# Interleaving scores and transposes in the attention of a hybrid decoder block, with smaller edits at the start, in the parameters and at the end

## The chip, the cores and the metric

The kernel runs on one core of one Trainium2 chip. The metric is the device time of one execution in microseconds (us), the median of several runs. All tensors are fp32. The core has a matrix engine (TensorE, "PE" in the profile, with its weight loads listed as "PEld"), VectorE (DVE), ScalarE (ACT), GpSimd (POOL) and SyncE (SP), which here only issues DMAs.

## The reference

The reference is one layer over 512 tokens of width 1024. Of it, what bears on the change:

```python
xn = rmsnorm(x, norm_g)                       # 512 x 1024
u  = xn @ w_in                                # all column groups of one projection
# mLSTM branch: q, k get a causal depthwise convolution of width 4 + SiLU; 4 heads of 256
q, k = silu(conv(u_q, conv_q_w, conv_q_b)), silu(conv(u_k, conv_k_w, conv_k_b))
ya = head_layernorm(mlstm(q, k, v, i, f)) * mh_norm_g * ...
# sparse attention branch: 8 heads of 64, 2 key groups; rotary angles on the first 16 of 64 dims
q, ks, kw = rope(u_nq), rope(u_nks), rope(u_nkw)
for each head, each of two key sets (selected, window):
    P = softmax(causal(q k^T / 8));  yb += gate * (P @ v)
yb += gate * compressed attention over 31 blocks
# both branches: silu gate, branch projection, sigmoid merge, one output projection
out = rmsnorm(x + merged @ w_out, final_norm_g)
```

The attention here is dense and causal for both key sets: 512 tokens fit in the window and in the selected blocks.

## The kernel before, in words

A matrix product of two fp32 matrices is done as three passes in TensorE's rounded fp32 format: each operand is split into a high part (a rounding copy, mostly on ACT) and a low part (a subtraction on DVE), and high x high, low x high and high x low are added up in one PSUM bank. `split` does this for one tile; names that end in `h` and `l` are the two parts. Weights arrive as `wr` (or `R`, `T`) and become `wh` and `wl`; `hTh` and `hTl` are the two parts of the normalized input, transposed.

The program has five stretches. From 0 to 26 us (first stage): four blocks of 128 tokens, `xts[0..3]`, are loaded; for each, `stats` finds the factor `r` of the norm (ACT squares, POOL power), `normed(tb, half)` scales half a block on DVE in place (`xt`), `turned` transposes it on TensorE, `high` and `low` split it. In between, a small projection (`small_hi`, `small_lo` split its weights `sraw` into `shi` and `slo`; `some_of` are its matmuls) gives value rows and gate columns, which `evacuate` takes out of PSUM. From 26 to 205 us: the projections for values and the gate paths, with sums for a Winograd scheme, and fitted into them two small jobs. `params` loads the convolution weights, the norm gains, the position table `cpos` and the positions, and transposes them on TensorE so that they lie along partitions (eight transposes of 11 rows into `prm`, two more). `angles` builds cosines and sines of the rotary angles, pads them to 128 columns a token block and transposes them (eight transposes of 128 by 128) into `Ct` and `St`, which the rotation of queries and keys reads from about 203 us on. From 205 to 380 us: the attention. From 380 to 525 us the mLSTM, from 525 us the branch and output projections, and the end.

The attention has 16 units (`units`: four pairs of heads, two heads, two key sets) of `NT` = 4 query blocks. For a block `qb`, `score` makes two matmuls into a `ps` bank (there are two), and `softmax_block` takes the minimum of the negated scores on DVE (the custom instruction) and the exponential with its sum on ACT, into the tile `P`. After a unit's last block DVE makes the reciprocal of the four sums and the gate (`st`), and POOL scales the four blocks of `P` (line 1058). `ptrans(P, kb)` then transposes key block `kb` of `P` for the query blocks that see it: 4, 3, 2, 1 transposes for `kb` 0 to 3, into a `pt` bank (there are two), which `split` copies to `pth` (ACT) and `ptl` (DVE). `pvmul` multiplies both by the values into the `po` bank (one), and `collect` takes a head's result out.

Between these, `tick(n)` runs `n` passes (the three-pass products' matmuls `pp<-hTh,wh`, `hTl,wh`, `hTh,wl`, 512 columns each) of a `stream` of other column projections, and one step of each side job (`compressed`, `mgate`). These "fill" matmuls are needed anyway: what is not done here is done by `stream.drain()` after the attention. The order on TensorE is the order of the code; ACT's, DVE's and POOL's is set by a scheduler that the program runs at build time, which is why rows are compared in the built program further down. All ACT, DVE and PE instructions carry the line of one recording helper, L75.

The loop of a unit: four times (score of the next unit, three fill passes, one late product), then four times (one `ptrans` of this unit, three fill passes, and the product that is `LAG` = 3 behind).

At the end, per token block, `join` adds a PSUM bank to `xo`, `square` squares it on ACT with a sum into `fs`, `more` adds the sum to `fb` on POOL, `factor` makes the power -1/2 in `fr` on POOL, and `times` (DVE, by the gain `late`), `scaled` (ACT, by `fr`) or `both` (DVE, one instruction for the two) give the output, which is stored.

Of the kernel before, what the change touches and what calls it, by code (L numbers as in the profile page):

```python
# [19 lines left out]
D = 1024  # L20
# [7 lines left out]
LAG = 3  # L28
# [30 lines left out]
def build(  # L59
# [45 lines left out]
    cpos = pers.tile([128, 32], F32, name="cpos")  # L105
# [6 lines left out]
    mhalf = pers.tile([128, 4], F32, name="mhalf")  # L112
# [120 lines left out]
    prm = pers.tile([128, 8, 11], F32, name="prm")  # L233
# [9 lines left out]
    vD = dram.tile([128, NT, D], F32, name="vD")  # L243
    gD = {
# [10 lines left out]
    posT = tiny[:, 256:260]  # L255
# [30 lines left out]
    with tc.tile_pool(name="ph0", bufs=2, side="right") as p0, tc.tile_pool(  # L286
# [8 lines left out]
        act.preload_act_table_set("natural_log_exp_and_others")  # L295
        ordered.add("pe")
# [12 lines left out]
        nc.sync.dma_start(cst[:, :CTRI], consts[:, :CTRI])  # L309
# [53 lines left out]
        bif = sp.tile([128, 8], F32, name="bif")  # L363
        bng = sp.tile([128, 24], F32, name="bng")
# [4 lines left out]
        def evacuate(tb, ps):  # L369
            pv = ps[:, 0:256].rearrange("p (b g d) -> p b g d", b=2, g=2)  # L370
            for b in range(2):
                split(pv[:, b], vsw[:, tb, b, :, 0, :], vsw[:, tb, b, :, 1, :])
            dve.tensor_tensor(gp[:, tb, 0:24], ps[:, 256:280], bng, OP.add)
            dve.tensor_tensor(gp[:, tb, 24:32], ps[:, 280:288], bif, OP.add)
# [44 lines left out]
        lo4, hi4 = range(4), range(4, 8)  # L419
        normed(0, 0)  # L420
# [4 lines left out]
        stats(1)  # L425
# [5 lines left out]
        low(0, 0)  # L431
# [5 lines left out]
        low(0, 1)  # L437
        small_hi(6, "p")
        high(1, 0)
        high(1, 1)  # L440
        small_hi(4, "a")
        small_lo(0)
        small_lo(2)
        low(1, 0)
        low(1, 1)
        some_of(0, "lh", lo4)
        some_of(1, "hh", lo4)
        some_of(0, "hh", hi4)
        some_of(0, "lh", hi4)
        some_of(1, "hh", hi4)  # L450
# [3 lines left out]
        some_of(1, "lh", hi4)  # L454
        whole(0, 0)
        whole(0, 1)
        stats(2)
        small_lo(6)
        small_lo(4)
        some_of(0, "hl", (6, 7, 4, 5), stop=True)  # L460
        some_of(1, "hl", (6, 7, 4, 5), stop=True)
        whole(1, 0)
        whole(1, 1)
        stats(3)
        nc.sync.dma_start(bif[:, 0:4], b_igate[0].partition_broadcast(128))
        nc.sync.dma_start(bif[:, 4:8], b_fgate[0].partition_broadcast(128))
        nc.sync.dma_start(bng, b_nsa_gate[0].partition_broadcast(128))
        for hf in range(2):
            normed(2, hf)
            turned(2, hf, PT())  # L470
        three = idle, PS()
        for hf in range(2):
            normed(3, hf)
            turned(3, hf, three[hf])
        vq = quarters(vview, ((0, 0), (1, 0)))
        for tb in (2, 3):
            for hf in range(2):
                high(tb, hf)
                low(tb, hf)
            if tb == 2:  # L480
                evacuate(0, sums[0])
# [5 lines left out]
        for tb in (2, 3):  # L487
            some_of(tb, "hh", lo4)
            some_of(tb, "hl", lo4)
            some_of(tb, "hh", hi4)  # L490
            some_of(tb, "hl", hi4)
            some_of(tb, "lh", lo4)
            some_of(tb, "lh", hi4, stop=True)
# [144 lines left out]
    def params():  # L638
        nc.sync.dma_start(cst[:, CTRI:], consts[:, CTRI:])
        rows = wn.tile([128, D], F32, name="zt", tag="zt")[:11]  # L640
        crow = tiny[:32, 384:512]
        pi = tiny[:4, 512:640].bitcast(I32)
        nc.sync.dma_start(pi, positions[0].rearrange("(a b) -> a b", a=4))
        nc.sync.dma_start(crow[0:16, :], cmp_pos_k[0].rearrange("(a b) d -> a (b d)", b=2))
        nc.sync.dma_start(crow[16:32, :], cmp_pos_v[0].rearrange("(a b) d -> a (b d)", b=2))
        r0 = 0
        for a in (conv_q_w, conv_q_b, conv_k_w, conv_k_b, mh_norm_g):
            src = a[0] if len(a.shape) == 3 else a
            nc.sync.dma_start(rows[r0 : r0 + src.shape[0], :], src)
            r0 += src.shape[0]  # L650
# [5 lines left out]
        pf = tiny[:4, 0:128]  # L656
        dve.tensor_copy(pf, pi)
        pe.transpose(ps[:, 128:132], pf, ident[:4, :4])
        dve.tensor_copy(prm, ps[:, 0:88].rearrange("p (k r) -> p k r", k=8))
        dve.tensor_scalar(prm[:, :, 10], prm[:, :, 10], 0.25, None, OP.mult)  # L660
        dve.tensor_copy(cpos, ps[:, 96:128])
        dve.tensor_copy(posT, ps[:, 128:132])

    def angles():
# [16 lines left out]
        for cc in (c1, c2, c3):  # L681
# [4 lines left out]
        pads = wn.tile([128, D], F32, name="zt", tag="zt")  # L686
        cpad, spad = (
            pads[:, o : o + 512].rearrange("p (b g d) -> p b g d", b=NT, g=2) for o in (0, 512)
        )
        pool.memset(cpad, 1.0)  # L690
        pool.memset(spad, 0.0)
        for g in range(2):
            for o in (0, 8):
                dve.tensor_copy(cpad[:, :, g, o : o + 8], sc[:, 1])
                dve.tensor_scalar(spad[:, :, g, o : o + 8], sc[:, 0], 1.0 if o else -1.0, None, OP.mult)
# [883 lines left out]
```

## Time and profile before

| | |
|---|---|
| runs of the kernel before | median 615.88 us of 3 (615.53 to 616.04) |
| the profiled execution | 615.5 us, of which 613.7 us span, 1.8 us around it |
| granted TensorE clock, mean | 0.997 |
| busy: PE / PEld / DVE / ACT / POOL | 599.9 / 499.6 / 483.7 / 344.1 / 61.8 us |
| attention, steady part 245 to 360 us | PE busy 113.61 of 115 us, DVE 85.51, ACT 72.39, POOL 26.63 |

The profile gives one execution. The time of an instruction in a row is from its start to its modelled end; matmuls are pipelined, so a matmul starts while the one before still shows as busy, and the distance of two starts is what a matmul costs TensorE. A bracket behind a row ("0.60 <-DVE ptl") is the idle time of that engine ahead of the instruction and the work that ended it.

### The profile page before, as it was taken

How to read it: one execution, taken by the hardware profiler on the slowest of the kernel's cores; microseconds unless marked ns; L12 is line 12 of the kernel's file. 1: busy time of each engine (PE TensorE's matmuls, PEld its weight loads, DVE VectorE, ACT ScalarE, POOL GpSimd, SP SyncE). 2: the span in 40 equal slices, each digit the busy share in tenths (PEclk: the TensorE clock that was granted, in tenths of full speed). 3: DMA queues.
4: the chain of work that ended last, by engine and by line, in shares of the span. 5: the costliest groups of instructions: out<-in, count | busy, mean ns of one | idle time of the engine just before them, and what ended most of it. 6: DMA issues, size and time to landing. Idle time of an engine off the chain costs nothing.

```text
span 613.7 us, 8639 instructions
## 1 busy us (share of the span) xinstructions
PE 599.9 (98%) x3024; PEld 499.6 (81%) x3024; DVE 483.7 (79%) x920; ACT 344.1 (56%) x641; POOL 61.8 (10%) x127
## 2 busy tenths in 40 slices
PE   8999999999999999999999999999999999999995
PEld 7988888888888877787878877888787878888884
DVE  6789898596686577885966586889898997589984
ACT  6664556564442356575756575565656563434564
POOL 3000000000100003222121212000000000010122
PEclk9999999999999999999999999999999999999998
DMA  7956554402068361323223222432232234990623
GB/s 223 361 156 187 172 155 137 138 0 87 18 171 219 78 172 57 87 57 85 57 69 91 65 68 87 119 88 69 69 116 92 78 90 127 308 254 18 206 52 139
DMA packets 83052, 73.99 MB, mean 121 GB/s; under 512 B 5072, under 2 KB 64628, under 8 KB 83008
## 3 DMA queue, kind: packets, MB, share of 16 engines
q1 hardware_dynamic: 81854, 70.81, 39.1%
q0 software_dynamic: 1008, 2.36, 2.1%
q8 instruction: 24, 0.39, 0.3%
q10 hardware_dynamic: 146, 0.27, 0.1%
q14 instruction: 20, 0.16, 0.1%
HBM read 61.23 MB, written 8.39 MB: 113 GB/s over the span
## 4 chain that ended last, share of the span: by engine, by line
PE 75%; DVE 15%; ACT 4%; issue 3%; POOL 2%; DMA 1%; POOLq 0%; DVEq 0%; SPq 0%; ACTq 0%
PE pp L75 43%; PE ps L75 18%; PE pt L75 10%; PE po L75 3%; DVE u L75 3%; DVE wl L75 2%; ACT wh L75 1%; DVE P L75 1%; DVE ptl L75 1%; POOL P L1058 1%; ACT P L75 1%; DVE xo L75 1%; DVE num L75 1%; DVE qkl L75 1%; DVE Th L75 1%
## 5 line engine op out<-in xcount | busy, mean ns | idle before, releaser
L75 PE MATMUL pp<-hTh,wh 128*128 128x512 f32 (+1 forms) x360 | 143.5, 399 | 0.0
L75 PE MATMUL pp<-hTl,wh 128*128 128x512 f32 (+1 forms) x360 | 140.0, 389 | 0.0
L75 PE MATMUL pp<-hTh,wl 128*128 128x512 f32 (+1 forms) x360 | 139.4, 387 | 0.0
L75 ACT ACTIVATE wh<-wr 128x1024 fp32r<-128x1024 f32 x56 | 59.0, 1057 | 58.3 <-PE pp L75 52.4
L75 DVE TENSOR_TENSOR wl<-wr,wh 128x1024 fp32r<-128x1024 f32 x56 | 68.2, 1219 | 19.1 <-ACT wh L75 19.0
L75 PEld LDWEIGHTS pp<-hTh,wl 128*128 128x128 f32 x360 | 67.7, 188 | 13.3
L75 PEld LDWEIGHTS pp<-hTh,wh 128*128 128x128 f32 x360 | 68.0, 189 | 10.5
L75 PEld LDWEIGHTS pp<-hTl,wh 128*128 128x128 f32 x360 | 68.0, 189 | 9.4
L1058 POOL TENSOR_SCALAR P<-P,st 128x128 f32<-128x128 f32 (+1 forms) x64 | 36.5, 590 | 157.1 <-DVE st L75 117.4
L75 DVE TENSOR_TENSOR wl<-T,wh 128x1024 fp32r<-128x1024 f32 x28 | 34.0, 1219 | 11.3 <-ACT wh L75 11.3
L75 DVE TENSOR_TENSOR ptl<-pt,pth 128x512 fp32r<-128x512 f32 (+1 forms) x64 | 30.2, 485 | 14.2 <-ACT pth L75 13.8
L75 ACT ACTIVATE P<-P,st 128x128 f32<-128x128 f32 (+3 forms) x64 | 35.5, 554 | 9.9 <-DVE st L75 9.2
L75 ACT ACTIVATE pth<-pt 128x512 fp32r<-128x512 f32 (+1 forms) x64 | 26.9, 434 | 24.6 <-PE pt L75 13.4
L75 DVE TENSOR_TENSOR wl<-R,wh 128x1024 fp32r<-128x1024 f32 x28 | 33.7, 1219 | 8.5 <-ACT wh L75 8.3
L75 DVE CUSTOM_DVE_ANT_0 P<-ps,cst 128x128 f32<-128x128 f32 (+3 forms) x64 | 30.4, 486 | 12.0 <-PE ps L75 11.7
L75 ACT ACTIVATE wh<-T 128x1024 fp32r<-128x1024 f32 x28 | 29.4, 1056 | 18.1 <-PE pp L75 11.0
L75 ACT ACTIVATE wh<-R 128x1024 fp32r<-128x1024 f32 x28 | 29.2, 1058 | 13.3 <-PE pp L75 5.8
L75 DVE SCALAR_TENSOR_TENSOR u<-pp,prm,u 128x511 f32<-128x511 f32 (+2 forms) x48 | 35.6, 742 | 0.4 <-ACT u L75 0.2
L75 PE MATMUL pt<-cst,P 128*128 128x128 f32 x160 | 29.0, 278 | 2.2 <-DVE ptl L75 1.1
L75 PEld LDWEIGHTS pt<-cst,P 128*128 128x128 f32 x160 | 19.7, 140 | 13.8 <-DVE ptl L75 7.5
L75 PE MATMUL ps<-k,Th 128*128 128x256 f32 (+2 forms) x112 | 28.9, 341 | 0.2 <-DVE st L75 0.2
L75 PE MATMUL pp<-yah,wh 128*128 128x512 f32 x64 | 25.0, 391 | 0.0
(350 smaller groups left out, 1348.0 us busy)
## 6 DMA issues: line engine op xcount, KB each, us to landing
wr<-w_in SPq DMA_DIRECT2D x44, 512.0 KB
R<-w_in SPq DMA_DIRECT2D x24, 512.0 KB
gD<-sg SPq DMA_DIRECT2D x16, 256.0 KB
s<-gD SPq DMA_DIRECT2D x16, 256.0 KB
wr<-w_branch_a SPq DMA_DIRECT2D x8, 512.0 KB
R<-w_out SPq DMA_DIRECT2D x8, 512.0 KB
vD<-cq SPq DMA_DIRECT2D x8, 256.0 KB
wr<-vD SPq DMA_DIRECT2D x4, 512.0 KB
```

The costliest lines, as they stand in the source:

```text
L75: ins = fn(*args, **kw)
L1058: pool.tensor_scalar(pj, pj, st[:, 2, j : j + 1], 1.0, OP.mult, OP.mult)
```

## The change

Four parts.

**Attention.** One loop over blocks in place of one over units with two inner loops: a score block, three fill passes, one `ptrans`, three fill passes, one product. The `ptrans` belongs to the block `NT + BEHIND` = 6 steps back, and products follow their transposes by `LAG` = 1 (2 where a head's bank is new). `P` has four buffers in place of three. In the last quarter of the scores one fill pass fewer is run per step, so that 12 passes move behind the attention (102 there, 90 before). The compressed attention's job waits six steps in place of three before its transposes, and the next pair's queries are begun in units 3, 7 and 11.

**Parameters.** The rows are loaded as one tile of 124 rows by 128, turned by one transpose, and `prm` becomes [128, 128] with the position table and the -1/2 constants in it. The cosines and sines are packed without padding (`cc`, 32 columns a token block), turned by one transpose, copied to SBUF by ACT, written to a DRAM tile `csD`, and read back into rows of `Ct` and `St` by four DMAs on SP's queue. `Ct` and `St` are filled with ones and zeros by POOL.

**First stage.** The load of the constants moves from SP's queue to ACT's; block 1 is normed straight after block 0; the small projection's matmuls stand in another order, with block 2's transposes ahead; three bias tiles become one and `evacuate` has one split and one add.

**End.** The last square with its sum is one DVE instruction (`last_factor`), which starts from `fb`, so that POOL goes straight to the power. Token block 0's second half is multiplied by the gain on DVE and scaled on ACT, in place of `both` on DVE; token block 1's second half is one `both` in place of two instructions.

```diff
-LAG = 3
+LAG = 1
+BEHIND = 2
+YIELDS = 6
...
-            at.tile([128, 1280], F32, name="P", tag="P", bufs=3),
+            at.tile([128, 1280], F32, name="P", tag="P", bufs=4),
...
-        for qb in range(NT):
-            if i + 1 < 16:
-                score(*units[i + 1], qb, pair)
-            tick()
-            if late:
-                late.popleft()()
-        for kb in range(NT):
-            tt = ptrans(cur[0], kb)
-            tick()
...
-            late.append(apply)
-            if len(late) > LAG:
-                late.popleft()()
+    for n in range(NT, last + NT + BEHIND):
+        u, m = n // NT, n - NT - BEHIND
...
+        if n < last:
+            scores(n)
+        tick(FILL - 1 if 3 * last // 4 <= n < last else FILL)
+        if m >= 0:
+            apply = values_of(m)
             tick()
+            late.append(apply)
+            while len(late) > (LAG + 1 if m % (2 * NT) == 1 else LAG):
                 late.popleft()()
...
-        for k in range(8):
-            pe.transpose(ps[:, k * 11 : (k + 1) * 11], rows[:, k * 128 : (k + 1) * 128], ident[:11, :11])
-        pe.transpose(ps[:, 96:128], crow, ident[:32, :32])
...
-        pe.transpose(ps[:, 128:132], pf, ident[:4, :4])
+        dve.tensor_copy(rows[96:100], pi)
+        pe.transpose(ps[:, :124], rows, ident[:124, :124])
...
-        for src, dst in ((cpad, Ct), (spad, St)):
-            ps = PP()
-            for tb in range(NT):
-                pe.transpose(
-                    ps[:, tb * 128 : (tb + 1) * 128], src[:, tb].rearrange("p g d -> p (g d)"), ident
-            A(dst, ps, AF.Copy)
+        ps, turned = PP(), tiny[:, 384:512]
+        pe.transpose(ps[:, :128], tiny[:, 512:640], ident)
+        A(turned, ps[:, :128], AF.Copy)
+        nc.sync.dma_start(csD, turned)
+        rows = csD.rearrange("(b r) t -> r b t", b=NT)
+        for g in (0, 64):
+            for r, dst in ((0, Ct), (16, St)):
+                nc.sync.dma_start(
+                    dst[g : g + 16].rearrange("p (b t) -> p b t", b=NT), rows[r : r + 16]
...
-        nc.sync.dma_start(cst[:, :CTRI], consts[:, :CTRI])
+        keep(nc.scalar.dma_start(cst[:, :CTRI], consts[:, :CTRI]))
...
+        stats(1)
         normed(0, 0)
         turned(0, 0, PT())
         warm(3)
         normed(0, 1)
         turned(0, 1, PT())
-        stats(1)
...
-        low(0, 0)
         normed(1, 0)
...
+        def last_factor(tb, cs, n):
+            xv, j = xo[:, tb, cs], junk[:, tb * 2 + n % 2, : cs.stop - cs.start]
+            v = fs[:, tb, n : n + 1]
+            dve.tensor_tensor_reduce(
+                out=j, in0=xv, in1=xv, scale=1.0 / D, scalar=fb[:, tb : tb + 1],
+                op0=OP.mult, op1=OP.add, accum_out=v,
+            )
+            keep(pool.tensor_tensor(fr[:, tb : tb + 1], v, mhalf[:, 0:1], OP.pow))
...
+        times(0, R)
         factor(0, 1)
         more(1, 1)
-        times(1, R0)
         scaled(0, L)
+        scaled(0, R)
         product((None, Y[2]), "MS4", w3, False, tbs=(1,), cs=halves_of[1])
         join(1, R1, Y[2][:, halves_of[1]])
-        square(1, R1, 2)
-        both(0, R)
-        store(0, R)
-        factor(1, 2)
+        last_factor(1, R1, 2)
         scaled(1, L, nc.scalar)
-        both(1, R1)
-        dve.tensor_scalar(xo[:, 1, R0], xo[:, 1, R0], fr[:, 1:2], None, OP.mult)
+        both(1, R)
         store(1, R)
```

In the built programs the recording helper is line 75 before and line 77 after. TensorE in the middle of the attention, before: the four groups of transposes of one unit (`pt<-cst,P`) with their fill.

```order
L75 MATMUL pt<-cst,P 128x128 x4
L75 MATMUL pp<-hTh,wh 128x512
L75 MATMUL pp<-hTl,wh 128x512
L75 MATMUL pp<-hTh,wl 128x512
L75 MATMUL pt<-cst,P 128x128 x3
L75 MATMUL pp<-hTh,wh 128x512
L75 MATMUL pp<-hTl,wh 128x512
L75 MATMUL pp<-hTh,wl 128x512
L75 MATMUL pp<-hTh,wh 128x512
L75 MATMUL pt<-cst,P 128x128 x2
```

The same engine and place in the changed kernel, with a product (`po`) and a score block (`ps`) between two groups of transposes.

```order
L77 MATMUL pt<-cst,P 128x128 x4
L77 MATMUL pp<-hTh,wh 128x512
L77 MATMUL pp<-hTl,wh 128x512
L77 MATMUL pp<-hTh,wl 128x512
L77 MATMUL po<-pth,vsw 128x128
L77 MATMUL po<-ptl,vsw 128x128
L77 MATMUL ps<-k_1609,Th 128x512
L77 MATMUL ps<-k_1610,Th 128x512
L77 MATMUL pp<-hTh,wh 128x512
L77 MATMUL pp<-hTl,wh 128x512
L77 MATMUL pp<-hTh,wl 128x512
```

Between two groups of transposes stood three or four fill passes; now stand six, a product and a score block. The product ahead of that score belongs to the unit before.

VectorE in the first stage, before (after its memsets): the norm of block 0, a low part, the norm of block 1.

```order
L75 SCALAR_TENSOR_TENSOR xt<-xt,r,ps 128x512 x2
L75 TENSOR_TENSOR hTl<-pt,hTh 128x4x128
L75 SCALAR_TENSOR_TENSOR xt<-xt,r,ps 128x512 x2
L75 TENSOR_TENSOR hTl<-pt,hTh 128x4x128
L75 TENSOR_TENSOR slo<-sraw,shi 128x576 x2
```

The same place now:

```order
L77 SCALAR_TENSOR_TENSOR xt<-xt,r,ps 128x512 x4
L77 TENSOR_TENSOR hTl<-pt,hTh 128x4x128
L77 TENSOR_TENSOR slo<-sraw,shi 128x576
L77 TENSOR_TENSOR hTl<-pt,hTh 128x4x128
L77 TENSOR_TENSOR slo<-sraw,shi 128x576
```

The four norm instructions stand together, and the first low part behind them.

VectorE's last instructions before:

```order
L75 SCALAR_TENSOR_TENSOR xo<-pp,xo 128x256
L75 TENSOR_TENSOR xo<-xo,late 128x256
L75 SCALAR_TENSOR_TENSOR xo<-pp,xo 128x256
L75 SCALAR_TENSOR_TENSOR xo<-xo,fr,late 128x512
L75 SCALAR_TENSOR_TENSOR xo<-xo,fr,late 128x256
L75 TENSOR_SCALAR xo<-xo,fr 128x256
```

And now, with the square and its sum as the two ISA rows:

```order
L77 SCALAR_TENSOR_TENSOR xo<-pp,xo 128x256
L77 TENSOR_TENSOR xo<-xo,late 128x512
L77 SCALAR_TENSOR_TENSOR xo<-pp,xo 128x256
L77 ISA junk,fs<-xo,fb 128x256
L77 ISA fs 128x1
L77 SCALAR_TENSOR_TENSOR xo<-xo,fr,late 128x512
```

The gain multiplication ahead of the last join is twice as wide, the square has come to VectorE, and one full-width instruction is left behind it.

More of the change, by code (lines that the diff above doesn't have):

```diff
@@ L110, in build @@
     ident = cst[:, CI : CI + 128]
-    mhalf = pers.tile([128, 4], F32, name="mhalf")
+    prm = pers.tile([128, 128], F32, name="prm")
+    cpos, posT, mhalf = prm[:, 0:32], prm[:, 96:100], prm[:, 124:128]
     pool.memset(mhalf, -0.5)
@@ L370, in evacuate @@
             pv = ps[:, 0:256].rearrange("p (b g d) -> p b g d", b=2, g=2)
[L371 to L374, printed above, removed]
+            split(pv, vsw[:, tb, :, :, 0, :], vsw[:, tb, :, :, 1, :])
+            dve.tensor_tensor(gp[:, tb], ps[:, 256:288], bias, OP.add)
         stats(0)
@@ L441, in build @@
         small_hi(4, "a")
+        small_hi(6, "p")
+        low(0, 0)
         small_lo(0)
+        low(0, 1)
         small_lo(2)
@@ L454, in build @@
         some_of(1, "lh", hi4)
+        stats(2)
         whole(0, 0)
         whole(0, 1)
[L457 to L461, printed above, removed]
+        stats(3)
         whole(1, 0)
         whole(1, 1)
[L464 to L467, printed above, removed]
-        for hf in range(2):
[L469 to L481, printed above, removed]
+        for o, b in ((0, b_nsa_gate), (24, b_igate), (28, b_fgate)):
+            nc.sync.dma_start(bias[:, o : o + b.shape[1]], b[0].partition_broadcast(128))
+        vq = quarters(vview, ((0, 0), (1, 0)))
+        normed(2, 0)
+        turned(2, 0, PT())
+        high(2, 0)
+        small_lo(4)
+        some_of(0, "hl", (4, 5))
+        some_of(1, "hl", (4, 5))
+        small_lo(6)
+        some_of(0, "hl", (6, 7), stop=True)
+        some_of(1, "hl", (6, 7), stop=True)
+        normed(2, 1)
+        turned(2, 1, PT())
+        high(2, 1)
+        some_of(2, "hh", lo4)
+        normed(3, 0)
+        turned(3, 0, idle)
+        some_of(2, "hh", hi4)
+        normed(3, 1)
+        turned(3, 1, PS())
+        low(2, 0)
+        low(2, 1)
+        evacuate(0, sums[0])
+        for hf in range(2):
+            high(3, hf)
+            low(3, hf)
         w1 = hilo(vq[0, 0])
@@ L487, in build @@
         for tb in (2, 3):
[L488 removed]
+            if tb == 3:
+                some_of(tb, "hh", lo4)
+                some_of(tb, "hh", hi4)
             some_of(tb, "hl", lo4)
[L490 removed]
             some_of(tb, "hl", hi4)
@@ L685, in angles @@
         A(sc, ang, AF.Sin)
[L686 to L695, printed above, removed]
+        cc = tiny[:, 512:640].rearrange("p (b r) -> p b r", b=NT)
+        for o in (0, 8):
+            dve.tensor_copy(cc[:, :, o : o + 8], sc[:, 1])
+            dve.tensor_scalar(cc[:, :, 16 + o : 24 + o], sc[:, 0], 1.0 if o else -1.0, None, OP.mult)
+        pool.memset(Ct, 1.0)
+        pool.memset(St, 0.0)
         A(gates, gp[:, :, 0:24], AF.Tanh, scale=0.5)
@@ L1013, in compressed @@
         dve.tensor_tensor(sc, sc, c01.unsqueeze(2).broadcast_to([128, NT, 2, 32]), OP.mult)
-        yield
-        yield
-        yield
+        for _ in range(YIELDS):
+            yield
         ptc = PP()
@@ L1105, in build, with scores @@
     side.append(compressed(0))
-    pair = new_p(), new_p()
-    for qb in range(NT):
-        score(*units[0], qb, pair)
+    pairs_ = {}
+    def scores(n):
+        u, qb = divmod(n, NT)
+        if u % 2 == 0 and qb == 0:
+            pairs_[u // 2] = new_p(), new_p()
+        score(*units[u], qb, pairs_[u // 2])
+    for n in range(NT):
+        scores(n)
         tick(START_FILL)
```

90 lines of the change are left out of this document (42 added, 48 removed).

## The prediction

> **What bounds the kernel now.** I read the page's busy shares first, then the busy time by stretch, then the waits of one stretch, then single stalls in the timeline.
>
> ```profile
> PE 599.9 (98%) x3024; PEld 499.6 (81%) x3024; DVE 483.7 (79%) x920; ACT 344.1 (56%) x641; POOL 61.8 (10%) x127
> ...
> 26.00:208.00 182.00, 182.00 (x869) 152.63 (x869) 143.47 (x204) 95.47 (x129) 3.04 (x11) 1.00 0.46 134
> 208.00:245.00 37.00, 35.67 (x176) 28.03 (x175) 25.74 (x70) 21.52 (x52) 4.88 (x8) 1.00 0.42 113
> 245.00:360.00 115.00, 113.61 (x615) 93.05 (x614) 85.51 (x230) 72.39 (x181) 26.63 (x47) 1.00 0.27 73
> ```
>
> The columns are the stretch, its length, busy time of PE, PEld, DVE, ACT and POOL, the clock and DMA. TensorE has no idle time from 26 to 208 us, at a clock of 1.00, and little elsewhere. So the time is TensorE's: it falls only by a matmul that goes, a stall that goes, or work before the first and after the last matmul. In the attention, the two waits of TensorE that the change aims at are these (us in total, times, longest):
>
> ```profile
> PEld pt L75 <- DVE ptl L75: 7.3, 16, 1.0
> ...
> PEld pt L75 <- POOL P L1058: 1.5, 4, 0.5
> ```
>
> The first row is of 245 to 360 us, the second of 208 to 245. They are waits of the weight load, and part of each is covered by the matmul that still streams. The longest one shows how much:
>
> ```profile
> 276.88 0.40 PE L75 MATMUL pp<-hTh,wl 128*128 128x512 f32 x1
> 277.12 0.40 PE L75 MATMUL pp<-hTh,wh 128*128 128x512 f32 x1
> 278.11 0.44 PE L75 MATMUL pt<-cst,P 128*128 128x128 f32 x2 [0.60 <-DVE ptl L75]
> ...
> L75 ACT ACTIVATE pth<-pt 128x512 fp32r<-128x512 f32 (+1 forms) x64 | 26.9, 434 | 24.6 <-PE pt L75 13.4
> L75 DVE TENSOR_TENSOR ptl<-pt,pth 128x512 fp32r<-128x512 f32 (+1 forms) x64 | 30.2, 485 | 14.2 <-ACT pth L75 13.8
> ```
>
> A 512-column matmul costs 277.12 - 276.88 = 0.24 us from start to start, though its row says 0.40. Here the next start came 0.99 us later, so 0.75 us were lost of a wait of 1.0. TensorE waited for the third group of transposes, because there are two `pt` banks and the first was not yet read out: ACT's copy (0.43 us on average) and DVE's subtraction (0.49 us), one after the other and each behind other work, took longer than the transposes and the four fill passes in between.
>
> **The attention.** Loss now in the middle: 7.3 - 16 x 0.24 = 3.5 us, if each wait is covered by one matmul's 0.24. In the changed order a bank is used again after six fill passes for each of two steps, with a score and a product: by the count of matmuls in the built program times 0.24 us, 3.5 to 5.5 us after its transposes, in place of 1.6 to 2.0. These stalls go: -3.5 us. Outside this stretch (start and tail of the attention) TensorE idles 37 - 35.67 = 1.3 us and a little, part of it on POOL.
>
> What is late next? First, products now follow their transposes after 2.8 to 3.4 us (nine fill passes and a score, by the same count) against 3.4 to 4.8 before; the split needs 0.43 + 0.49 us, and with what is queued ahead up to about twice or three times that, so a few will be late by tenths: I give back 0.4. Second, the start of the attention: the first unit's scaling ends when it ends, and fewer matmuls stand ahead of its transposes: 0.5 given back. Third, the tail, where POOL has least time: 0.4. Net 3.5 - 1.3 = 2.2 us, between 0 (all of it becomes other waits) and 4.5 (also the 1.3 us of the first part go, and nothing is given back less 0.3).
>
> The give-backs rest on POOL's chain from a unit's last score to its first transposes:
>
> ```profile
> 323.52 0.68 PE L75 MATMUL ps<-k,Th 128*128 128x512 f32 x2
> ...
> 324.48 0.68 DVE L75 CUSTOM_DVE_ANT_0 P<-ps,cst 128x512 f32<-128x512 f32 x1
> ...
> 325.20 0.72 ACT L75 ACTIVATE P<-P,st 128x512 f32<-128x512 f32 x1 [0.53 <-DVE st L75]
> ...
> 326.05 0.18 DVE L75 RECIPROCAL st<-st 128x4 f32<-128x4 f32 x1 [0.88 <-ACT P L75]
> ...
> 326.62 2.06 POOL L1058 TENSOR_SCALAR P<-P,st 128x128 f32<-128x128 f32 x4 [5.10 <-ACT pth L75]
> ```
>
> From 323.52 to 326.62 + 2.06 = 328.68: 5.2 us, with little queued on DVE and ACT. Before, some 10 us of matmuls stood between these two points. In the new order 21 fill passes (21 x 0.24 = 5.0), six transposes (0.1 each), three products and three scores stand there: about 7.1 to 8.7 us in the middle, and about 6.5 in the last quarter, where each step has one fill pass fewer. So the chain still fits, with 2 us to spare and not 5. The 12 passes moved behind the attention cost nothing there and save nothing here: TensorE runs them either way. The fourth buffer of `P` adds no wait. `compressed` waiting six steps is hidden by the fill.
>
> One rule speaks against this:
>
> ```profile
> 231.61 1.22 DVE L75 TENSOR_TENSOR wl<-wr,wh 128x1024 fp32r<-128x1024 f32 x1
> 231.95 2.81 POOL L1058 TENSOR_SCALAR P<-P,st 128x128 f32<-128x128 f32 x4 [51.40 <-DVE st L75]
> ...
> L1058 POOL TENSOR_SCALAR P<-P,st x64: 374/590/1133, 232.0 to 373.4; 128x128 f32<-128x128 f32 x16, 128x256 f32<-128x256 f32 x16, 128x384 f32<-128x384 f32 x16, 128x512 f32<-128x512 f32 x16
> ```
>
> The last row gives shortest, median and longest in ns. The four scalings took 2.81 us beside a `wl` subtraction and 2.06 us above: 0.75 us more. The Trainium skill ("SBUF — State Buffer", Who interferes with whom) says that VectorE and GpSimd share one pair of memory ports under an exclusive lock, so that one holds the other up for a whole instruction. This row agrees as far as one case can. By that rule a chain that meets one 1.22 us subtraction takes 6.4 us, still inside 7.1; the sum stays, and the rule counts under the third rival.
>
> **The start.**
>
> ```profile
> 8.04 0.57 POOL L357 TENSOR_TENSOR r<-v,mhalf 128x1 f32<-128x1 f32 x1
> 8.32 0.69 DVE L75 TENSOR_TENSOR hTl<-pt,hTh 128x512 fp32r<-128x512 f32 x1 [0.72 <-ACT hTh L75]
> 8.93 1.40 DVE L75 SCALAR_TENSOR_TENSOR xt<-xt,r,ps 128x512 f32<-128x512 f32 x2
> ...
> 9.73 0.66 PE L75 MATMUL pp<-cst,xt 128*128 128x128 f32 x4 [0.81 <-DVE xt L75]
> ```
>
> TensorE waits 0.81 us for block 1's norm. Its factor is there at 8.04 + 0.57 = 8.61, but DVE does block 0's low part first, till 9.0. With the norm ahead it can start at 8.65, 0.3 us earlier. The low part comes 1.4 us later, and the matmuls that read it stand later too in the new order; the cover is the `hh` matmuls of blocks 0 and 1. If that cover is short, nothing is gained. So -0.3 us, between 0 and the whole 0.81 and some of the 2.4 us idle before 26 us, at most 1.2. The constants' load on another queue moves nothing that TensorE waits for; the merged split and add relieve DVE and ACT, which do not bind there.
>
> **Parameters.**
>
> ```profile
> 69.58 0.66 PE L75 MATMUL pp<-cst,zt 11*128 11x11 f32 x8
> ...
> 70.29 0.50 PE L75 MATMUL ps<-wh,hTh 128*128 128x512 f32 x1
> ...
> 81.31 1.03 PE L75 MATMUL pp<-cst,zt 128*128 128x128 f32 x8
> 82.10 0.48 PE L75 MATMUL pt<-wh,S4h 128*128 128x512 f32 x1
> ...
> 80.65 9.37 SPq L622 DMA_DIRECT2D vD<-cq  x4
> 95.60 0.39 SPq L266 DMA_DIRECT2D R<-w_in  x1
> ...
> xo<-late POOLq DMA_DIRECT2D x5, 256.0 KB, 3.3
> ```
>
> Starts count, on an engine with no idle time: the ten small transposes (with the positions') take 70.29 - 69.58 = 0.71 us, eight big ones 82.10 - 81.31 = 0.79, so one takes 0.10. One in place of ten: -0.6; one in place of eight: -0.7. Both are sure to count, unless TensorE comes to wait for the conversion of the positions, a small DVE instruction now ahead of the one transpose (loads were begun a step earlier). The way through DRAM is one write and four reads on SP's queue. No row has such a small one; the nearest landing is 3.3 us for 256 KB, so two hops are estimated at under 6.6 us. SP waits from 90.0 to 95.6 with its next weight load, and `Ct` is read near 203 us: hidden, cost 0. If the queue were held, R would be late by a few us; then the 0.7 is lost and more.
>
> **The end.**
>
> ```profile
> 606.38 0.28 PE L75 MATMUL pp<-wh,mSl 128*128 128x256 f32 x1
> ...
> 606.67 0.43 DVE L75 TENSOR_TENSOR xo<-xo,late 128x256 f32<-128x256 f32 x1 [0.86 <-ACT junk L75]
> 607.02 0.42 DVE L75 SCALAR_TENSOR_TENSOR xo<-pp,xo 128x256 f32<-128x256 f32 x1
> 607.10 0.19 POOL L1446 TENSOR_TENSOR fb<-fb,fs 128x1 f32<-128x1 f32 x1
> 607.17 0.72 ACT L75 ACTIVATE xo<-xo,fr 128x512 f32<-128x512 f32 x1 [0.53 <-POOL fr L1450]
> ...
> 607.80 0.40 ACT L75 ACTIVATE junk<-xo 128x256 f32<-128x256 f32 x1
> ...
> 608.70 0.55 POOL L1450 TENSOR_TENSOR fr<-fb,mhalf 128x1 f32<-128x1 f32 x1
> ...
> 609.29 0.49 DVE L75 SCALAR_TENSOR_TENSOR xo<-xo,fr,late 128x256 f32<-128x256 f32 x1 [1.20 <-POOL fr L1450]
> ...
> 610.04 0.40 ACTq L1453 DMA_DIRECT2D out<-xo  x1
> ```
>
> Now the last join ends at 607.44, the ACT square at 608.20, two small steps follow, and the power runs 608.70 to 609.25. After: the join ends about 607.3 (the wider gain multiplication is done earlier), `fb` is there at 607.29; the square on DVE, at the price of a two-input row of this width (0.43) and a sum (0.09), ends 607.85; POOL's 0.55 with its start delay gives the factor at about 608.55, 0.7 earlier. ACT is behind two full scalings (607.17 + 2 x 0.72 = 608.61) and ends at 609.35; DVE's `both` at full width ends then too. The last store issues 0.65 us earlier. Ends: 0.4 (the new instruction is dearer) and 0.85 (the join comes first).
>
> **The sum.** 2.2 + 0.3 + 0.6 + 0.7 + 0.65 = 4.45 us. The profiled execution took 615.5 us (span 613.7 and 1.8 around it), so 611.05; it lies 0.4 under the median of the runs, 615.88, so I predict 611.4.
>
> **Rivals.** (1) The attention gains nothing: products, closer behind their transposes, wait in place of the transposes. For it: DVE is busy 85.5 of 115 us and has backlogs. Against: the distance is still near three times the pure need. Only the other 2.25 us remain: 613.6. (2) All goes: also the start's 1.2, 0.85 of the end, and 4.5 in the attention, with the parameters' 1.3 in all 7.85: 608.0. Against: the 1.3 us at the start of the attention hang on POOL's scaling, which the change does not shorten. (3) Slower: POOL's chain outlasts its window in every unit. With twelve windows of 7.9 us on average and four of 6.5, it decides from a mean chain of 7.9 us: four units lose 1.4 each, 5.6 in sum, which eats the 3.5 + 2.25 of the rest. At 8.2 us, 12 x 0.3 + 4 x 1.7 = 10.4 are lost, and the time is 615.9 - 5.75 + 10.4 = 620.5. For it: DVE queues the subtractions of 1.22 us, which hold the chain's DVE steps and, as seen, POOL; three in a row would do. Against: 5.2 undisturbed, and more room on ACT. (4) The order changes nothing in sum: the attention costs 2 us by mixed small waits, about 615.5.
>
> **How the numbers follow.** Forecast (609.5 to 613): 0.62. Rival 1 (613 to 614.8): 0.18, of which 0.05 count as no change. Rival 2: 0.10. Rival 3: 0.07. Rival 4: 0.03. About 0.2%, 1.2 us, is what a measurement of this kernel can tell from no change; so faster is below 614.65: 0.62 + 0.13 + 0.10 = 0.85; same 0.08; slower 0.07. The range from 608.2 to 614.6 leaves out half of rival 2, a part of rival 1, and 3 and 4: under 0.2.
>
> **What would show it.** Right: no "pt <- DVE ptl" wait of weight loads over 0.5 us in the middle of the attention; TensorE's count of transposes down by 16; the last store issued 0.65 us closer to the last matmul; a wait of 0.5 us at about 9 us. Wrong: new waits "po <- DVE ptl", or "pt <- POOL P" in many units, of more than 3 us in sum; a wait for R or wr behind the round trip near 95 us; rotation waiting for `Ct`.

## The result and the profile after

The changed kernel takes 612.62 us (median of 4 runs, 612.24 to 613.2) against 615.96: a ratio of 0.995, interval 0.9937 to 0.9963, some 3.3 us. The forecast was 611.4. The profiled execution has a span of 610.4 us, 3.3 less than before, so that the two traces can account for the difference to a tenth.

The page's busy shares after, then two stretches of the attention (columns as before: stretch, length, PE, PEld, DVE, ACT, POOL):

```profile
PE 596.2 (98%) x3008; PEld 499.5 (82%) x3008; DVE 483.1 (79%) x906; ACT 343.2 (56%) x635; POOL 63.4 (10%) x126
...
243.00:358.00 115.00, 114.97 (x638) 97.17 (x637) 89.05 (x240) 75.38 (x190) 27.45 (x48) 1.00 0.27 75
358.00:378.00 20.00, 18.48 (x97) 14.56 (x96) 12.92 (x32) 11.72 (x26) 5.35 (x8) 1.00 0.22 67
```

In the middle of the attention TensorE is now busy all the time; in the last 20 us it has lost 1.5 us. The waits of TensorE and its weight loads from 222 to 380 us say on what:

```profile
PEld pt L77 <- POOL P L1055: 4.7, 9, 1.3
PE pt L77 <- POOL P L1055: 2.5, 5, 1.0
PEld po L77 <- DVE ptl L77: 0.9, 4, 0.3
```

The wait "pt <- DVE ptl" of 7.3 us is gone. What waits now is the transposes for POOL's scaling, at the start and at the tail.

Where the time went can be read from the starts of matmuls that are the same in both programs. Before:

```profile
25.95 0.40 PE L75 MATMUL ps<-wh,hTh 128*128 128x512 f32 x1
...
223.67 0.48 PE L75 MATMUL ps<-k,Th 128*128 128x256 f32 x2
...
403.70 0.47 PE L75 MATMUL ps<-qkh,qkh 128*128 128x512 f32 x1
```

and after, the last row being the last matmul of the program (before at 606.38):

```profile
25.96 0.40 PE L77 MATMUL ps<-wh,hTh 128*128 128x512 f32 x1
...
222.20 0.35 PE L77 MATMUL ps<-k,Th 128*128 128x256 f32 x1
...
400.55 0.47 PE L77 MATMUL ps<-qkh,qkh 128*128 128x512 f32 x1
...
603.16 0.28 PE L77 MATMUL pp<-wh,mSl 128*128 128x256 f32 x1
```

| stretch (from, to) | before, us | after, us | change | term of the prediction |
|---|---|---|---|---|
| start of the trace to first Winograd matmul | 25.95 | 25.96 | 0.0 | -0.3 |
| from there to the first score (holds the parameters) | 197.72 | 196.24 | -1.5 | -1.3 |
| first score to the first mLSTM score, fill included | 180.03 | 178.35 | -1.7 | -2.2 |
| from there to the last matmul | 202.68 | 202.61 | -0.1 | 0 |
| start of the last matmul to the end of the span | 7.32 | 7.24 | -0.1 | -0.65 |
| sum | 613.70 | 610.40 | -3.3 | -4.45 |

For the attention I also added up, matmul by matmul, the distance of two starts less what that width costs where nothing waits (0.227 us for 512 columns of a three-pass product, in proportion for fewer, 0.109 for a transpose). It was 0.87 us from the first score to the first transposes before and 1.98 after, 11.89 and 7.57 from there to the last score, and 1.12 and 2.69 from there to the last product: the start lost 1.1 us, the middle won 4.3, the tail lost 1.6. In the middle, the gaps just ahead of a transpose alone fell from 5.7 to 2.1 us, which is most of the 4.3.

Two counts in the traces show why the ends lost. The chain of a unit is the time from the start of its last score matmul to the end of POOL's fourth scaling. The window is what TensorE has to do in between: the matmuls between that score and the unit's first transposes, each at what it costs where nothing waits.

| units | fill passes in the window, before and after | window before, us | window after, us | chain before, us | chain after, us |
|---|---|---|---|---|---|
| 1 | 14, 11 | 4.7 | 3.5 | 6.6 | 6.6 |
| 2 to 12 | 27, 21 (18 in one) | 9.6 to 10.3 | 7.2 to 8.0 | 4.9 to 8.2 | 4.6 to 7.3 |
| 13 | 24, 17 | 8.9 | 6.3 | 5.8 | 4.8 |
| 14 | 24, 17 | 9.4 | 6.8 | 8.3 | 7.1 |
| 15 | 13, 7 | 6.4 | 4.1 | 7.7 | 5.1 |
| 16 | 10, 9 | 4.9 | 4.2 | 4.7 | 6.8 |

The transposes start as each block of `P` is scaled, so a chain a little longer than its window costs nothing: units 2 to 14 have no wait for POOL. The first and the last two units have, and their chains are no longer than others; their windows are short, since few fill passes stand in them. At the tail the fill runs out: counted in the code, the stream holds 366 passes when the attention begins (13 jobs of 24 passes, less 18 that are done, and the gate projections of the first three pairs of heads), and the steps up to unit 15's last score ask for just as many. The last pair's gate projection joins only with the last product. The trace agrees: the third pair's projection leaves its bank at 359.2 us, and the passes behind that are the last pair's (taken out at 376.0), which the build pulled forward. For TensorE's order is not quite the code's; here too a score stands between the two matmuls of one product, which follow each other in the code.

```profile
352.16 0.33 PE L77 MATMUL po<-pth,vsw 128*128 128x384 f32 x1
352.33 0.28 PE L77 MATMUL ps<-k,Th 128*128 128x256 f32 x1
352.64 0.44 PE L77 MATMUL po<-ptl,vsw 128*128 128x384 f32 x1
```

### The profile page after: what moved, and what is told of

Read it like the earlier page. It is cut to its first block, busy times and chain, and to the rows that moved or that the text cites. A ratio compares the mean times of both kernels' runs of the same rounds, so it can differ in the third digit from the quotient of the medians.

```text
span 610.4 us, 8577 instructions
## 1 busy us (share of the span) xinstructions
PE 596.2 (98%) x3008; PEld 499.5 (82%) x3008; DVE 483.1 (79%) x906; ACT 343.2 (56%) x635; POOL 63.4 (10%) x126
## 5 line engine op out<-in xcount | busy, mean ns | idle before, releaser
L1055 POOL TENSOR_SCALAR P<-P,st 128x128 f32<-128x128 f32 (+1 forms) x64 | 38.1, 615 | 152.5 <-DVE st L77 134.4
L77 ACT ACTIVATE wh<-T 128x1024 fp32r<-128x1024 f32 x28 | 29.4, 1057 | 18.4 <-PE pp L77 10.3
```

The lines of the kernel that those rows point to most:

```text
L77: ins = fn(*args, **kw)
L1055: pool.tensor_scalar(pj, pj, st[:, 2, j : j + 1], 1.0, OP.mult, OP.mult)
```

## The experiments

Gains are against runs of the kernel before on the same chip. The first stage's length scatters between profiles (the first Winograd matmul starts between 25.4 and 26.9 us over all of them), so differences of a few tenths are read from the rest of the trace.

**The four parts, each alone on the kernel before.** Edits: the attention's loop, `P` buffers and waits of `compressed`; the packed parameters and `csD`; the first stage; the end.

> The kernel before with the attention part alone. My reading of the two traces (same markers in both: the first score and the first convolution matmul of the mLSTM) gives the attention 1.7 us: 4.3 won between the first transposes and the last score, 1.1 lost at its start and 1.5 at its tail. So 614.2 us. The prediction's term was 2.2: 613.7. If the parts lean on one another (the scheduler mixes them), the gain is under 1 us: above 615.0.

Measured: 614.29 us, ratio 0.9976 (0.9966 to 0.9986), a gain of 1.5. In its trace the same pieces stand as in the full change: 1.95, 7.49 and 2.68 us over the bare work. So the attention is worth 1.5 to 1.7 us, and no lean on another part is seen.

> The kernel before with the parameters' part alone. Reading of the traces: 1.5 us between the end of the first stage and the first score, of which the prediction had 1.3. So 614.4 to 614.6. A rival: part of the 1.5 comes from fill passes that moved across the first score, then 0.9 or less: 615.0 or more.

Measured: 614.88 us, ratio 0.9983 (0.9974 to 0.9992). The trace from the first Winograd matmul to the first score has 196.19 us in place of 197.72, the 1.5 again; the timed gain of 0.9 is lower, and its interval (0.5 to 1.6) holds both readings. The rival is excluded by the trace, not by the time: from the first score to the first mLSTM score it is 179.9 us, as before.

> The kernel before with the first-stage part alone. Reading of the traces: 0 (the first Winograd matmul starts at 25.95 us before and 25.96 after), so 615.9. The prediction's term was 0.3: 615.6. In the profile the second block's factor should again be ready at 9.2 us, 0.6 later than before, because the constants' load, moved to another queue and issued earlier, shares the DMA engines with the first two blocks of x.

Measured: 615.66 us, ratio 1.0 (0.9991 to 1.0008): no difference. The second block's factor was ready at 9.11 us.

> The kernel before with the end part alone. Reading of the traces: 0.1 us of span after the last matmul in place of the prediction's 0.65, so 615.8 against 615.2. In the profile POOL's first addition into fb should take 0.69 us beside the wider gain multiplication on VectorE, and the last square should wait for it about 0.5 us.

Measured: 615.91 us, ratio 0.9999 (0.999 to 1.0008): no difference. POOL's addition took 0.70 us and the last square waited 0.53.

By time the four parts add up to 2.3 us, against 3.3 for all together. Most of the difference is not in the program's own span. A time is the span and some time around it, and that rest is 1.9 to 2.2 us in every execution of these four kernels, against 1.7 to 1.9 in those of the kernel before and of all others; why stays open. By the mean of the spans the parts gain 1.7 (attention), 1.3 (parameters), 0.3 (start) and 0.2 us (end), each give or take 0.3: some 3.5 in sum. So the start and the end are small gains that the times alone don't show.

**The constants' load.**

```diff
-        keep(nc.scalar.dma_start(cst[:, :CTRI], consts[:, :CTRI]))
...
+        nc.sync.dma_start(cst[:, :CTRI], consts[:, :CTRI])
         nc.sync.dma_start(xts[1], x[0, 128:256, :])
```

> The changed kernel with the constants' load back on SP's queue, behind the first block of x; the new order of the norms stays. If the shared DMA engines held up the first blocks of x, the second block's factor is ready at about 8.6 us in place of 9.2, its norm starts there, and the first stage ends 0.2 to 0.5 us earlier than 25.96: 612.2 us against 612.6. If the loads don't matter, the factor stays near 9.2 and the time at 612.6.

Measured: 612.01 us, ratio 0.9941 (0.9926 to 0.9956), 0.6 under the changed kernel, though the intervals overlap. The rows of its start, to be held against those of the changed kernel below it:

```profile
8.02 0.57 POOL L360 TENSOR_TENSOR r<-v,prm 128x1 f32<-128x1 f32 x1
8.63 1.41 DVE L77 SCALAR_TENSOR_TENSOR xt<-xt,r,ps 128x512 f32<-128x512 f32 x2 [1.20 <-POOL r L360]
...
25.36 0.40 PE L77 MATMUL ps<-wh,hTh 128*128 128x512 f32 x1
```

```profile
8.62 0.57 POOL L360 TENSOR_TENSOR r<-v,prm 128x1 f32<-128x1 f32 x1
9.22 1.41 DVE L77 SCALAR_TENSOR_TENSOR xt<-xt,r,ps 128x512 f32<-128x512 f32 x2 [1.30 <-POOL r L360]
```

The norm does start as soon as its factor is there, as meant, but the factor is later. Over all 14 profiles the first block's factor is ready at 5.9 to 6.4 us in the seven with the load on SP's queue, behind the first block of x, and at 6.5 to 7.4 in the seven with it on ACT's: that shift, 0.9 us between the medians, is the load's. For the second block the two groups overlap (8.6 to 9.8 and 9.0 to 9.8), so most of the 0.6 us that I read from two profiles was scatter; what the load costs in the end lies between 0 and 0.6. The traces show how: with the load on ACT's queue the constants' packets of 512 bytes run from about 3 us to between 4.8 and 6.2, in the midst of those of x, and ACT's second square of the first block, from whose start to the factor it is 1.7 us in both kernels, starts at 4.8 to 5.7 us in place of 4.2 to 4.7.

The new order of the norms did gain what was forecast. From the second block's factor to the first Winograd matmul it is 17.2 to 17.4 us in the five profiles with the old order and 16.8 to 16.9 in the nine with the new one, 0.4 us less between the medians. The scatter of the factor hides this in the time of a single profile.

**The end.**

```diff
-        times(0, R)
...
-        scaled(0, R)
...
         last_factor(1, R1, 2)
+        both(0, R)
+        store(0, R)
```

> The changed kernel without the wide gain multiplication ahead of the last join: the second half of block 0 goes through one VectorE instruction behind the last square again. If that multiplication held POOL's addition (0.69 us in place of 0.19) and by it the last square, the addition takes 0.19 again, the square does not wait, and the last store is issued 2.9 us after the start of the last matmul in place of 3.35: 612.2 us. If POOL is late for another reason, the square still waits 0.5 us and the time is 612.6.

Measured: 612.8 us, ratio 0.9951 (0.9934 to 0.9967): no gain. Its trace, after that of the changed kernel:

```profile
603.05 0.69 DVE L77 TENSOR_TENSOR xo<-xo,late 128x512 f32<-128x512 f32 x1 [0.46 <-ACT junk L77]
603.10 0.69 POOL L1459 TENSOR_TENSOR fb<-fb,fs 128x1 f32<-128x1 f32 x1 [2.22 <-ACT junk L77]
...
604.61 0.48 DVE L77 CUSTOM_DVE_ANT_0 junk<-xo,fb 128x256 f32<-128x256 f32 x1 [0.53 <-POOL fb L1459]
...
605.18 0.55 POOL L1472 TENSOR_TENSOR fr<-fs,prm 128x1 f32<-128x1 f32 x1 [0.60 <-DVE fs L77]
...
606.51 0.38 ACTq L1475 DMA_DIRECT2D out<-xo  x1
```

```profile
603.70 0.19 POOL L1459 TENSOR_TENSOR fb<-fb,fs 128x1 f32<-128x1 f32 x1 [2.22 <-ACT junk L77]
...
605.12 0.75 DVE L77 SCALAR_TENSOR_TENSOR xo<-xo,fr,late 128x512 f32<-128x512 f32 x1
605.28 0.99 POOL L1472 TENSOR_TENSOR fr<-fs,prm 128x1 f32<-128x1 f32 x1 [0.61 <-DVE fs L77]
```

The first expectation held for the addition (0.69 us beside the VectorE multiplication, 0.19 without it) and failed for the sum: now the power stands beside a VectorE instruction of that kind and takes 0.99 us in place of 0.55, and the square still waits 0.21 us, since the addition it needs stands behind the other block's power on POOL. The last store is issued 3.3 us after the last matmul's start, as in the changed kernel. In the first case POOL's addition ends 0.05 us after the VectorE instruction beside it (603.79 and 603.74), in the second the power ends 0.40 us after it (606.27 and 605.87). All but 0.15 us of what POOL's instruction takes alone comes after VectorE's end. Beside a join, which has one of its two tensors in PSUM, the same power takes its usual 0.55 us (at 603.87 us in the changed kernel). That fits what the Trainium skill ("SBUF — State Buffer", Who interferes with whom) says of the port pair that the two engines share: one holds the other up for a whole instruction. Here it is seen on POOL instructions of 128 elements.

**The last quarter's fill passes.**

```diff
-        tick(FILL - 1 if 3 * last // 4 <= n < last else FILL)
+        tick(FILL)
```

> The changed kernel with three fill passes in the last quarter of the scores too. If the tail's loss is a window too short for the softmax chain that ends in POOL, TensorE's stalls between 358 and 378 us (2.5 us over its bare work) fall to about 1.3, and the time to 611.4. If the fill passes bring so much splitting work to VectorE that the chain gets longer by the same, the stalls stay at 2 us or more: 612.4 to 612.8.

Measured: 612.77 us, ratio 0.9955 (0.994 to 0.997): no gain, the second expectation. TensorE's waits for POOL over the attention stay:

```profile
PEld pt L77 <- POOL P L1055: 4.5, 10, 1.2
PE pt L77 <- POOL P L1055: 2.0, 5, 1.0
```

In the last unit POOL's scaling took only 2.06 us here, but it ended as long after the last score (364.8 to 371.8) as in the changed kernel (362.9 to 369.7). That the passes' splitting lengthened the chain is not shown, though, for the run did not make the windows it was meant to make. In the last two units 5 and 12 passes stand in the window in place of 7 and 9 (3.6 and 5.0 us of work in place of 4.1 and 4.2), and the chains are 6.2 and 7.0 us in place of 5.1 and 6.8. By the count above, three passes in place of two in each of these steps empty the stream two steps earlier. What the run shows is that a larger number of passes a step did not widen the windows that were short.

**The start of the attention.**

```diff
+        if m < 0:
+            tick()
         if m >= 0:
             apply = values_of(m)
```

> The changed kernel with three more fill passes in each of the two steps that have no transposes yet. TensorE now loses 1.75 us at 230 to 232.5 us waiting for POOL's first scaling; six passes are 1.4 us of work that is needed anyway. If only cover was missing, the stalls fall to 0.4 and the time to 611.3. If the passes' splitting delays the chain, the gain is under 0.5: 612.2 or more.

Measured: 612.82 us, ratio 0.9952 (0.9938 to 0.9967): no gain. The stall in front of the transposes fell from 1.75 to 0.9 us, but a tick also steps the side jobs, and one of their matmuls now came before VectorE had its input:

```profile
240.87 0.38 PE L77 MATMUL pp<-cst,cs 128*4 128x128 f32 x2 [0.55 <-DVE cs L77]
```

In a second kernel the added line is `stream.step(FILL)`, which runs the passes alone.

> The changed kernel with three more fill passes in the two steps without transposes, but no step of the side jobs with them (the earlier kernel with both lost 0.7 us to a side job's matmul that came before VectorE had its input). If that was all, POOL's stalls at the start stay at 0.9 us in place of 1.75 and nothing is lost behind: 611.8 us. If the extra passes' splitting delays other work, the new stalls come elsewhere: 612.4 or more.

Measured: 611.93 us, ratio 0.9938 (0.9923 to 0.9953), as the first expectation had it. The stall is 0.9 us, the wait for `cs` is gone. The interval still holds the second expectation's 612.4, so it is the trace that decides. In both kernels the first unit's window has 17 passes in place of 11, 4.9 us of work in place of 3.5: here more fill did help.

**Who scales P.**

```diff
             for j in range(NT):
                 pj = P[:, POFF[j] : POFF[j] + (j + 1) * 128]
-                pool.tensor_scalar(pj, pj, st[:, 2, j : j + 1], 1.0, OP.mult, OP.mult)
+                if j > 1 and (c, hh, b) in ((0, 0, 0), (3, 1, 0), (3, 1, 1)):
+                    A(pj, pj, AF.Copy, scale=st[:, 2, j : j + 1])
+                else:
+                    pool.tensor_scalar(pj, pj, st[:, 2, j : j + 1], 1.0, OP.mult, OP.mult)
```

> The changed kernel with ScalarE scaling the two larger blocks of P in the first and the last two units, POOL the two smaller ones. If the length of POOL's scaling (2.8 us in the first and the last unit, against 2.06 undisturbed) is what TensorE waits for there, the stalls by POOL (1.75 us at the start, 2.7 at the tail) fall by about 2 us in all: 610.6 us. If the chain ahead of the scaling is the longer part, or ScalarE's queue holds its share up, they fall by under 0.7: 612 or more.

Measured: 610.44 us, ratio 0.9913 (0.9897 to 0.993), 2.2 under the changed kernel. The last unit in the changed kernel, from its last score to its first transposes:

```profile
362.88 0.45 PE L77 MATMUL ps<-k,Th 128*128 128x512 f32 x1
...
363.14 0.69 DVE L77 TENSOR_TENSOR ptl<-pt,pth 128x512 fp32r<-128x512 f32 x1
...
363.75 0.68 DVE L77 CUSTOM_DVE_ANT_0 P<-ps,cst 128x512 f32<-128x512 f32 x1
...
364.35 0.94 ACT L77 ACTIVATE pth<-pt 128x384 fp32r<-128x384 f32 x2
...
365.18 0.72 ACT L77 ACTIVATE P<-P,st 128x512 f32<-128x512 f32 x1
...
366.11 0.41 DVE L77 TENSOR_TENSOR ptl<-pt,pth 128x256 fp32r<-128x256 f32 x1
...
366.51 1.22 DVE L77 TENSOR_TENSOR wl<-wr,wh 128x1024 fp32r<-128x1024 f32 x1
366.79 2.86 POOL L1055 TENSOR_SCALAR P<-P,st 128x128 f32<-128x128 f32 x4 [4.76 <-PE po L77]
...
368.02 0.78 PE L77 MATMUL pt<-cst,P 128*128 128x128 f32 x2 [0.69 <-POOL P L1055]
```

The score ends at 363.3; the minimum waits behind a `ptl` till 363.75, the exponential behind two `pth` copies till 365.18, the gate's multiplication behind another `ptl` till 366.44, and the scaling lies beside a `wl` subtraction and takes 2.86 us. Together 6.8 us from 362.88. With the work shared:

```profile
358.00:378.00 20.00, 20.00 (x106) 16.27 (x105) 13.96 (x33) 14.43 (x31) 1.66 (x4) 1.00 0.30 88
...
367.02 1.23 ACT L77 ACTIVATE P<-P,st 128x384 f32<-128x384 f32 x2 [0.42 <-DVE st L77]
367.12 0.83 POOL L1058 TENSOR_SCALAR P<-P,st 128x128 f32<-128x128 f32 x2 [6.71 <-DVE st L77]
```

The scaling takes 1.23 us and TensorE is busy for the whole 20 us of the tail. But that the shorter scaling did this by itself is not shown. In unit 15 the chain is 4.0 us in place of 5.1, in unit 16 it is 6.65 (361.60 to 368.25) in place of 6.8, hardly shorter. What changed as much is TensorE's order: the build laid 10 and 14 fill passes into these two windows in place of 7 and 9, which makes them 5.2 and 6.0 us in place of 4.1 and 4.2. At the start, where the window stayed at 3.5 us, one stall of 1.15 us remains, ahead of the first block's transposes.

**Spacing without interleaving.** On the kernel before:

```diff
                 score(*units[i + 1], qb, pair)
-            tick()
+            tick(1)
...
             tt = ptrans(cur[0], kb)
-            tick()
+            tick(5)
```

> The kernel before with its two inner loops as they were, but one fill pass behind each score block and five behind each group of transposes, the same sum. If the middle's stalls came from too little work between transposes that share two banks, the weight loads' wait for ptl (7.3 us in 16) falls under 2 and the time by 1.5 to 3 us, without any interleaving of scores and transposes: 613 to 614.3. If the interleaving itself is needed, because four score blocks in a row with little between them wait for their own two banks, new waits of the score matmuls take the gain: 615.3 or more.

Measured: 615.53 us, ratio 0.9996 (0.9986 to 1.0005): no difference. Its largest waits of TensorE, 222 to 382 us:

```profile
PEld pt L75 <- POOL P L1058: 2.5, 6, 0.8
PEld po L75 <- ACT pth L75: 2.1, 6, 0.5
PEld pt L75 <- DVE ptl L75: 1.9, 5, 0.7
```

The wait for `ptl` fell from 7.5 (in this stretch) to 1.9 us, so the stalls did come from too little work between groups that share two banks. But the time did not follow: products and the scaling wait instead, and not the scores, as I had expected of the rival. By the gaps between starts, the middle won 1.6 us (2.8 ahead of transposes, less 0.9 lost ahead of products) and the tail lost 1.2. This way of moving the same passes about is not enough; the change's order, in which score blocks too stand between transposes, keeps the gain. No run separates that order from what came with it, the shorter `LAG`, the fourth buffer of `P` and the later start of the compressed attention's transposes.

**Together.** The constants' load back, ScalarE's share, and the passes without side jobs.

> The changed kernel with three edits together: the constants' load back on SP's queue, ScalarE's share of the scaling in the first and the last two units, and the six fill passes more before the first transposes (without the side jobs). If they act apart: 612.6 less 2.2, less 0.6, less 0.7 is 609.1 us, and the one stall of 1.15 us that was left before the first transposes is gone. If the extra passes and ScalarE's share hinder one another at the start, as they use the same engines, 609.9 or more.

Measured: 608.57 us (608.28 to 609.04), ratio 0.9886 (0.987 to 0.9903) to the kernel before, 4 us under the change. That is 0.5 us more than the edits' single gains add up to, so they do not hinder one another. Ahead of the transposes no stall of more than 0.35 us is left; the first window and the last two are now 4.9, 5.2 and 6.0 us.

```profile
222.00:380.00 158.00, 157.54 (x857) 132.07 (x857) 122.14 (x328) 105.72 (x261) 32.14 (x60) 1.00 0.26 75
```

## Why the prediction was right, and where it was off

The sign and the range held, and the forecast's mechanism was the one that acted: the transposes' wait for their banks went, and POOL's scaling took part of it back. It was 1.2 us too far down, and the total owes something to luck, as errors of both signs met in the attention. Term by term:

- **Parameters** (1.3): 1.5 up to the first score by the trace, 1.3 by the span, 0.9 by time. One transpose each is left, and the way through DRAM was hidden: the four reads were issued by 86.7 us and SP's next weight load waited till 94.2.

```profile
69.50 0.27 PE L77 MATMUL pp<-cst,tiny 124*128 124x124 f32 x1
...
80.56 0.27 PE L77 MATMUL pp<-cst,tiny 128*128 128x128 f32 x1
...
86.28 0.42 SPq L720 DMA_DIRECT2D St<-csD  x1
...
94.22 3.24 SPq L269 DMA_DIRECT2D R<-w_in  x2
```

- **Attention** (2.2): 1.7 by the trace and the span, 1.5 by time, and both sides of it were larger than said. The middle won 4.3 in place of 3.5 less 0.4: the listed waits, less what a streaming matmul covers, were too small a measure of it, and the sum of all gaps is the fuller one. The start lost 1.1 in place of 0.5, and the tail 1.6 in place of 0.4. Two steps failed there, and the second weighs more. The chain's length of 5.2 us (4.9 as the table above counts it) was read from one of the shortest units: in the same trace it runs from 4.7 to 8.3 us, 6.6 on average, and after the change it is 5.8 on average. And the window of about 6.5 us in the last quarter supposed that the stream would still have passes to give: it holds for units 13 and 14 (6.3 and 6.8), but units 15 and 16 have 4.1 and 4.2 us, and unit 1 has 3.5. In units 2 to 14 chains of up to 7.3 us cost nothing. In the last unit the chain took 6.8, since three of its links stood behind a `pth` or `ptl` of the unit before and the scaling ran beside a `wl`. I had priced that last point at 0.75 to 1.2 us and left it out of the sum because 6.4 is less than 7.1; in the tail the window was not 7.1. The third rival, slower by POOL's chain, was the right mechanism in the wrong number of units: three of sixteen, and there by the window more than by the chain.
- **Start** (0.3): 0 by time and 0.3 by the span with this part alone. The norms' new place gains 0.4 from the second factor on. That the load "moves nothing that TensorE waits for" was the wrong step: it holds up the first block's factor by 0.9 us, and the second's by something between 0 and 0.6, which comes off that gain. In the two profiles of the table the factor's lateness eats all of it.
- **End** (0.65): 0.1 in the table, 0.2 by the span with this part alone. The last store's issue came 0.3 us nearer to the last matmul; the rest was lost as POOL's addition, 0.5 us longer, was held by the widened gain multiplication, which I had taken as done earlier at no cost. The stores themselves cost little. The last column is GB/s; before, then after:

```profile
609.00:610.00 1.00, 0.00 (x0) 0.00 (x0) 0.71 (x2) 0.71 (x1) 0.26 (x1) 0.75 1.02 383
610.00:611.00 1.00, 0.00 (x0) 0.00 (x0) 0.04 (x1) 0.01 (x1) 0.00 (x0) 0.50 0.25 92
611.00:612.00 1.00, 0.00 (x0) 0.00 (x0) 0.00 (x0) 0.00 (x0) 0.00 (x0) 0.50 1.00 379
612.00:613.00 1.00, 0.00 (x0) 0.00 (x0) 0.00 (x0) 0.00 (x0) 0.00 (x0) 0.50 0.29 105
```

```profile
605.78:606.78 1.00, 0.00 (x0) 0.00 (x0) 0.73 (x1) 0.70 (x2) 0.00 (x0) 0.88 0.76 283
606.78:607.78 1.00, 0.00 (x0) 0.00 (x0) 0.00 (x0) 0.00 (x0) 0.00 (x0) 0.50 1.03 381
607.78:608.78 1.00, 0.00 (x0) 0.00 (x0) 0.00 (x0) 0.00 (x0) 0.00 (x0) 0.50 0.99 375
608.78:609.78 1.00, 0.00 (x0) 0.00 (x0) 0.00 (x0) 0.00 (x0) 0.00 (x0) 0.50 0.04 10
```

Before, the four last stores ran in two bursts with a pause; after, 1 MB runs in one. But the last packet moves 2.42 us after the last store's issue in place of 2.37, so 0.25 us of the 0.3 are kept up to there. What takes most of it back stands behind the last packet: 1.51 us to the end of the span in place of 1.31. Over the 14 traces this rest is 1.31 to 1.33 us in the five kernels without the parameters' part (the end part alone is one of them) and 1.50 to 1.62 in the nine with it, where SyncE runs three more of its semaphore instructions, 0.06 us apart, after the last packet. So 0.2 us of the missing gain is a cost of the parameters' part, which the prediction put at nothing; why those instructions come so late there stays open.

Of the signs named beforehand, two of those for right came: no "pt <- DVE ptl" wait is left, and TensorE's count fell by 16 (3024 to 3008). The wait at about 9 us is 0.78 us at 10.0 and not 0.5, and the last store came 0.3 us nearer and not 0.65. One sign of wrong came in part: 4.7 us of weight loads' waits "pt <- POOL P", but in three units and not in many.

## What to carry to other kernels

When the order of a bound engine is loosened so that one stall goes, the slack is taken from somewhere. Compare the next chain with its window in the place where the window is shortest (here the first and the last units): take the chain from several units with their queues, not from one undisturbed, and count in the built program what really stands in the window. More fill a step helped at the start and not at the tail, where there was no fill left to give; what is wanted there has to be saved before. An edit of one engine's work, as the shared scaling, can also move another engine's instructions, so the order has to be read again after each. And a load that is issued earlier on a free queue still shares the DMA engines with the one that is waited for.

## What was unexpected of the hardware

A POOL instruction on 128 elements took 0.69 and 0.99 us in place of 0.19 and 0.55 when a VectorE instruction with two tensors in SBUF as inputs ran beside it, and ended only after it. Beside one with a single input in SBUF the 0.55 stayed 0.55. Four 256 KB stores issued between about 605.2 and 606.5 us left at 375 to 381 GB/s together, and the last of them was hardly later for it: 2.42 us from issue to last packet in place of 2.37. A part of the kernel that ends before the first score, the parameters, added 0.2 us behind the last packet of the program.
